# Second block of a two-block network: low parts of the weights and half of the position additions moved to GpSimd, and the stick-breaking mask moved from the weights to the scores

## The chip, the cores and the metric

The kernel runs on one core of a Trainium2 chip. The metric is the device time of one execution in microseconds (us), as the median of several runs. TensorE (PE, its weight loads PEld), VectorE (DVE), ScalarE (ACT), GpSimd (POOL) and SyncE (SP, which issues the DMAs) each run their own fixed list of instructions and wait for each other through semaphores.

## The reference, cut to what matters

One sequence of 512 rows and 1024 columns goes through two blocks. The first is a root-mean-square norm, sliding-window attention and a gated convolution, and a feed-forward layer. The second projects the normed rows to 33 groups of columns and runs three mixers on them, whose results are projected, added and normed once more. Of the second block, the parts that the change touches are these:

```
h = x @ w_in                                              # 33 weight tiles of 128 columns, the gates with 18
kc, vc: blocks = src[:, blk_idx] + cmp_pos                # 31 blocks of 32 rows, a step of 16
        gelu(blocks @ w1) @ w2                            # compressed keys, compressed values
...
mask = s_idx[None, :] < t[:, None]                        # stick-breaking: strictly earlier keys
log_rest = where(mask, log_sigmoid(-z), 0)
between = reverse cumulative sum of log_rest, moved by one
a = where(mask, exp(log_sigmoid(z) + between), 0)
o = a @ v
...
hgrn2: gated linear recurrence in chunks of 64, 6 heads in 3 pairs
```

## The kernel before, in words

Everything is held transposed, with columns on the 128 partitions and the 512 rows along the free dimension. Each product with a weight is made of three matmuls per 128 by 128 piece, since both sides are split into a high part and a low part of what the high part leaves: high by high, high by low, low by high. A weight tile is 128 partitions by 8 pieces of 128, fetched by SP as `raw`. `split_w` (L223) makes `wh` by a copy on ACT (L230) and `wl = raw - wh` by a subtraction on DVE (its helper `tt`, L138). `raw`, `wh` and `wl` have two buffers each. The class `Weights` (L237) loads four tiles and splits two tiles ahead of the product, `dense`, which takes one: 24 matmuls of 128x512 for a whole tile. `W2` (L704) is its instance for the second block's projection: 32 whole tiles and one of 128x8x18 for the gates.

The last norm of the first block is that of `norm3`, which stands ahead of the first product of `W2` that leaves its bank. Its squares are summed tile by tile on GpSimd by `Squares.add` (L328); then `rms_scale` multiplies the sum by a matrix of ones on PE into bank `gb` (`pgb<-nk,ones`) and DVE reads that (L315). At the same time `load_biasc` (L878) copies 24 small strided pieces of the bias on GpSimd. It stands in `compressed`, which then calls `blocks` (L880) for the compressed keys (`kc`) and for the compressed values (`vc`). `blocks` adds the position table to strided views of the projected tile: 8 additions of 64 partitions by 8 by 31 on DVE (L899) for each of the two. The products that read them are first-layer matmuls `pgb<-np,nk`.

Stick-breaking, `sticks` (L1071), handles two heads at a time in two calls (`bq`, `bk`, `bv` with c 0 and 1), each with two heads and three score tiles `zs` per head that hold the four column bands of the lower triangle (`ZP`). Per tile: scores on PE into bank `ga`, a copy on ACT, then `e = log(1+exp(z))` in three ACT steps and one DVE step; `strict` (L1069, GpSimd `affine_select`) sets `e` to 0 where the key is not strictly earlier than the query; ACT copies the high part (L1100), DVE the low part; PE sums it with the triangular matrix `trir`; DVE adds the sums to the scores; ACT takes the exponential (L1116); `strict` once more sets the same part of the result to 0; and `run(todo, ends)` issues the products with the values (`poa<-lv,gp`) behind the last of these (`ends`).

The recurrence (`recurrence`, pairs g0, g1, g2) is the part with the most DVE and ACT instructions; its products stand between those of the projection. The Tile framework's scheduler sets the order of all engines when the program is built, by its own estimate and by priorities: `split_w` asks for a priority ahead of its place (`offset=100`), `run` for a higher one (1000). So the order of every engine is fixed in the program, and a change in one place can move instructions in another.

Of the kernel before, what the change touches and what calls it, by code (L numbers as in the profile page):

```python
# [10 lines left out]
F32 = mybir.dt.float32  # L11
# [3 lines left out]
AF = mybir.ActivationFunctionType  # L15
ALU = mybir.AluOpType
AX = mybir.AxisListType

P = 128
# [3 lines left out]
NEG = -1e30  # L23
# [26 lines left out]
IN2 = {}  # L50
for _n, _c in (("nq", 3), ("kc", 0), ("vc", 0), ("ks", 0), ("vs", 0), ("kw", 0), ("vw", 0), ("bq", 2), ("bk", 2),
               ("bv", 2), ("gq", 3), ("gf", 3), ("gi", 3), ("z", 8)):
    for _i in range(max(_c, 1)):
# [4 lines left out]
ORDER = [("gf", 0), ("gq", 0), ("gi", 0), "ng", "kc", "vc", ("nq", 0), ("nq", 1), ("nq", 2), "ks", "vs", "kw", "vw",  # L58
         ("gf", 1), ("gq", 1), ("gi", 1), ("bq", 0), ("bk", 0), ("bv", 0), ("gf", 2), ("gq", 2), ("gi", 2),
         ("bq", 1), ("bk", 1), ("bv", 1)]  # L60
# [8 lines left out]
def tile_net(ctx, tc, a, out):  # L69
# [64 lines left out]
    def stt(o, i0, s, i1, op0, op1):  # L134
        V.scalar_tensor_tensor(o, i0, s, i1, op0, op1)  # L135

    def tt(o, i0, i1, op):
        V.tensor_tensor(o, i0, i1, op)  # L138
# [81 lines left out]
        nc.sync.dma_start(raw, src)  # L220
        return raw

    def split_w(raw, cuts=(0, 8)):  # L223
        nk, w = raw.shape[1], raw.shape[2]
        wh = wp.tile([P, 8, P], F32R, tag="wh", name=nm("wh"), bufs=2)[:, :nk, :w]
        wl = wp.tile([P, 8, P], F32R, tag="wl", name=nm("wl"), bufs=2)[:, :nk, :w]
        with tc.high_priority(offset=100):
            for c0, c1 in zip(cuts, cuts[1:]):
                c = slice(c0, min(c1, nk))
                A.copy(wh[:, c], raw[:, c])  # L230
                tt(wl[:, c], raw[:, c], wh[:, c].bitcast(F32), ALU.subtract)
        return wh, wl

    class Weights:


        def __init__(self, srcs):  # L237
            self.srcs, self.raw, self.w, self.n = srcs, [], [], 0

        def ahead(self, loads, splits):  # L240
            while len(self.raw) < min(loads, len(self.srcs)):
                self.raw.append(fetch(*self.srcs[len(self.raw)]))
            while len(self.w) < min(splits, len(self.raw)):
                self.w.append(split_w(self.raw[len(self.w)]))

        def take(self):
            n = self.n
# [89 lines left out]
    raw = raw_tile()  # L337
# [20 lines left out]
    def C(n):  # L358
        o, w = CM[n]
        return cst[:, o:o + w]  # L360
# [340 lines left out]
        lower_bounds()  # L701


    W2 = Weights([(a["w_gate"], 8, 18) if key == "ng" else (a["w_in_2"][IN2[key]], 8) for key in ORDER])  # L704
    cmi = cp.tile([P, 2, P], U8, tag="cmi", name="cmi")
    cmf = tl("nk")[:, 0:256]
    nc.sync.dma_start(cmf, a["cmask"])
# [169 lines left out]
                o = 31 + 128 * (3 - i)  # L877
                G.tensor_copy(v[:, h, 0:n], bias[h][:, o:o + 16 * (n - 1) + 1:16])  # L878

    def blocks(name, w1name, w2name):  # L880

        w1 = [np_().rearrange("p (k h) -> p k h", k=4) for _ in range(4)]
        for n in range(4):
            nc.sync.dma_start(w1[n], a[w1name][:, 4 * n:4 * n + 4])
        w2 = small(64)
        nc.sync.dma_start(w2, a[w2name])
        yield from need(name)
        src = pr[name]
        blks = [nk(), nk()]
        pos = S("pos").rearrange("p (r j) -> p r j", r=2)  # L890
        for n in range(2):
            G.memset(blks[n][:, 496:512], 0.0)
            blk = blks[n][:, 0:496].rearrange("p (j n) -> p j n", j=8)
            for g in range(2):
                s = src[64 * g:64 * g + 64]
                for par in range(2):
                    v = bass.AP(tensor=s.tensor, offset=s.offset + par + 16 * n,
                                ap=[list(s.ap[0]), [2, 8], [16, 31]])
                    last = V.tensor_tensor(  # L899
                        blk[64 * par:64 * par + 64, :, 31 * g:31 * g + 31], v,  # L900
                        pos[64 * g:64 * g + 64, par, 8 * n:8 * n + 8].unsqueeze(2).to_broadcast([64, 8, 31]), ALU.add,
                    )
        yield 0
        return w1, w2, blks, last
# [6 lines left out]
    def compressed():  # L911
        for h in range(3):
            G.memset(vcn[h].rearrange("p g d -> p (g d)"), 0.0)
        load_biasc()
        wk1, wk2, bk, e0 = yield from blocks("kc", "w_ck1", "w_ck2")
        wv1, wv2, bv, e1 = yield from blocks("vc", "w_cv1", "w_cv2")

        ps = bank("gb")
        todo = []
        for k in range(16):  # L920
            c = slice(62 * (k % 8), 62 * (k % 8) + 64)
            for r, w1, blks in ((0, wk1, bk), (64, wv1, bv)):
                todo.append(later(ps[r:r + 64, 0:P], blks[k // 8][:, c], w1[k // 4][:, k % 4], k == 0, k == 15))
        run(todo, [e0, e1])
        xy = nk()
        x, y, yT = (xy[:, P * n:P * n + P] for n in range(3))
        A.copy(x, ps[:, 0:P])
        tt(y, x, x, ALU.mult)
        V.tensor_scalar(y, y, 0.044715, 1.0, ALU.mult, ALU.add)
        tt(y, y, x, ALU.mult)  # L930
        V.tensor_scalar(y, y, -2.0 * math.sqrt(2.0 / math.pi), 80.0, ALU.mult, ALU.min)
        A.activation(y, y, AF.Exp)
        V.tensor_scalar(y, y, 1.0, None, ALU.add)
        V.reciprocal(y, y)
        tt(y, y, x, ALU.mult)
        yield 2.0
        ps = bank("gb")
        TE.transpose(ps[:, 0:P], y, ident)
        A.copy(yT, ps[:, 0:P])
        ps = bank("gb")  # L940
        for g in range(2):
            for r in (0, 64):
                mm(ps[r:r + 64, 32 * g:32 * g + 31], wk2, yT[:, 31 * g:31 * g + 31])
        kv = ps[:, 0:64].rearrange("p (g n) -> p g n", g=2)[:, :, 0:31]
        A.copy(kc2[:, :, 0:31], kv)
        tt(kc2[:, :, 31:62], kv, kc2[:, :, 0:31].bitcast(F32), ALU.subtract)
        yield 0.3
        ps = bank("gb")
        for g in range(2):
            for h in range(3):  # L950
                mm(ps[32 * h:32 * h + 31, 64 * g:64 * g + 64], yT[:, 64 + 31 * g:64 + 31 * g + 31], wv2)
        for h in range(3):
            A.copy(vcn[h][32 * h:32 * h + 31], ps[32 * h:32 * h + 31, 0:128])
        yield 0.5
        yield from need("ng", ("nq", 0), ("nq", 1), ("nq", 2))
        for i in range(4):
            pc = small(192)
            pv = pc.rearrange("p (h n) -> p h n", n=32)[:, :, 0:31]
            st = small(16)
            ps = bank("gb")  # L960
            for g in range(2):
                for h in range(3):
                    n = 64 * (3 * g + h)
                    mm(ps[:, n:n + 62], pr["nq", h][g][:, i * P:(i + 1) * P], kc2[:, g, 0:62])
            sv = ps[:, 0:384].rearrange("p (h n) -> p h n", h=6)
            tt(pv, sv[:, :, 0:31], biasc[i], ALU.add)
            tt(pv, pv, sv[:, :, 31:62], ALU.add)
            V.tensor_reduce(st[:, 0:6], pv, AX.X, ALU.max)
            tt(pv, pv, st[:, 0:6].unsqueeze(2).to_broadcast([P, 6, 31]), ALU.subtract)
            A.activation(pv, pv, AF.Exp)  # L970
            V.tensor_reduce(st[:, 6:12], pv, AX.X, ALU.add)
            V.reciprocal(st[:, 6:12], st[:, 6:12])
            tt(st[:, 6:12], st[:, 6:12], gate[:, i].rearrange("p (h b) -> p h b", b=3)[:, :, 0], ALU.mult)
            tt(pv, pv, st[:, 6:12].unsqueeze(2).to_broadcast([P, 6, 31]), ALU.mult)
            G.memset(pc.rearrange("p (h n) -> p h n", n=32)[:, :, 31:32], 0.0)
            yield 0.7
            ps = bank("gb")
            for g in range(2):
                TE.transpose(ps[0:96, g * P:(g + 1) * P], pc[:, 96 * g:96 * g + 96], ident)
            if i % 2 == 0:  # L980
                pch = tl("np")
            o = pch[:, 256 * (i % 2):256 * (i % 2) + 256]
            A.copy(o[0:96], ps[0:96, 0:256])
            pcT.append(o.rearrange("p (g t) -> p g t", g=2))
            yield 0.3
        done.add("cmp")
# [79 lines left out]
    ZW = [512, 512, 256]  # L1066

    def strict(t, o):
        return G.affine_select(t[:, o:o + P], t[:, o:o + P], [[1, P]], ALU.is_gt, 0.0, base=0, channel_multiplier=-1)  # L1069

    def sticks(cs):  # L1071
        for c in cs:
# [4 lines left out]
            for hh in range(2):  # L1077
# [5 lines left out]
                for b in range(3):  # L1083
# [12 lines left out]
                    stt(e, z, 0.0, e, ALU.max, ALU.add)  # L1096
                    for jb in range(4):
                        if ZP[jb][0] == b:
                            strict(e, ZP[jb][1])
                    A.copy(sh[b], e)  # L1100
                    tt(sl[b], e, sh[b].bitcast(F32), ALU.subtract)
                    yield 0.8
                for b in range(3):
# [9 lines left out]
                            mm(cb[:, o + n - n2:o + n], w, sh[b2][:, o2:o2 + n2], jj == jb, False)  # L1113
                            mm(cb[:, o + n - n2:o + n], w, sl[b2][:, o2:o2 + n2], False, jj == 3)
                    tt(zs[b], zs[b], cb[:, :ZW[b]], ALU.add)
                    A.activation(zs[b], zs[b], AF.Exp)  # L1116
                    for jb in range(4):
                        if ZP[jb][0] == b:
                            e = strict(zs[b], ZP[jb][1])
                            if hh == 1:  # L1120
                                ends.append(e)
                    yield 0.8
                both.append(zs)
            todo = []
# [366 lines left out]
```

## Time and profile before

| what | value |
|---|---|
| median of 3 runs | 1061.83 us (1061.65 to 1062.62) |
| the profiled execution | 1061.65 us |
| its span in the trace | 1059.8 us |
[...]
| PE busy | 97% |
| DVE busy | 66% |
| ACT busy | 46% |
| GpSimd busy | 4% |

The span is the time from the first to the last instruction in the trace; the execution's time holds 1.9 us more around it. Busy is the time in which an engine carries out an instruction. PE's busy share hides where it stands still: the view of waits sums up the idle time of an engine by what ended it.

### The profile page before, as it was taken

How to read it: one execution, taken by the hardware profiler on the slowest of the kernel's cores; microseconds unless marked ns; L12 is line 12 of the kernel's file. 1: busy time of each engine (PE TensorE's matmuls, PEld its weight loads, DVE VectorE, ACT ScalarE, POOL GpSimd, SP SyncE). 2: the span in 40 equal slices, each digit the busy share in tenths (PEclk: the TensorE clock that was granted, in tenths of full speed). 3: DMA queues.
4: the chain of work that ended last, by engine and by line, in shares of the span. 5: the costliest groups of instructions: out<-in, count | busy, mean ns of one | idle time of the engine just before them, and what ended most of it. 6: DMA issues, size and time to landing. Idle time of an engine off the chain costs nothing.

```text
span 1059.8 us, 14588 instructions
## 1 busy us (share of the span) xinstructions
PE 1028.5 (97%) x5689; PEld 835.7 (79%) x5689; DVE 704.3 (66%) x1307; ACT 485.6 (46%) x854; POOL 47.4 (4%) x93
## 2 busy tenths in 40 slices
PE   9999999999999999999999999998999999999997
PEld 7788888888888888888877888766777777777886
DVE  6886643356448767777763333497779788788847
ACT  5764443322345444444442223342455477478830
POOL 0000000000220000000000111200000011001100
PEclk9999999999999999999999999999999999999999
DMA  6212232233432333333336333610221111011232
GB/s 221 80 61 80 80 100 80 100 100 103 155 110 91 100 100 99 100 94 90 97 99 208 95 100 104 222 61 24 88 69 61 40 53 49 22 60 41 71 110 79
DMA packets 32800, 97.83 MB, mean 92 GB/s; under 512 B 4878, under 2 KB 5390, under 8 KB 32732
## 3 DMA queue, kind: packets, MB, share of 16 engines
q1 hardware_dynamic: 32732, 96.91, 28.9%
q8 instruction: 44, 0.72, 0.3%
q14 instruction: 24, 0.20, 0.1%
HBM read 94.77 MB, written 5.27 MB: 94 GB/s over the span
## 4 chain that ended last, share of the span: by engine, by line
PE 73%; DVE 14%; ACT 6%; DMA 2%; issue 2%; POOL 1%; SPq 1%; POOLq 0%; DVEq 0%; ACTq 0%
PE pm L141 44%; PE poa L141 12%; PE pob L141 11%; PE pgb L141 3%; PE pga L141 2%; DVE wl L138 2%; DVE lv L138 2%; DVE dk L138 2%; DVE hk L138 1%; ACT wh L230 1%; DMA raw<-in_w_down 1%; DVE r L138 1%; DVE nk L1010 1%; DVE nk L899 1%; DVE nk L997 1%
## 5 line engine op out<-in xcount | busy, mean ns | idle before, releaser
L141 PE MATMUL pm<-x,wh 128*128 128x512 f32 x1360 | 435.2, 397 | 1.9 <-ACT x L287 1.0
L141 PEld LDWEIGHTS pm<-x,wh 128*128 128x128 f32 x1360 | 252.0, 189 | 56.2 <-issue 4.9
L230 ACT CAST wh<-raw 128x1024 fp32r<-128x1024 f32 (+2 forms) x153 | 156.5, 1024 | 256.7 <-issue 102.5
L141 PE MATMUL pm<-x,wl 128*128 128x512 f32 x680 | 268.3, 395 | 0.0
L138 DVE TENSOR_TENSOR wl<-raw,wh 128x1024 fp32r<-128x1024 f32 (+2 forms) x153 | 182.0, 1190 | 88.0 <-ACT wh L230 85.0
L141 PEld LDWEIGHTS pm<-x,wl 128*128 128x128 f32 x680 | 128.2, 188 | 27.5 <-issue 1.9
L141 PE MATMUL pob<-x,wh 128*128 128x512 f32 (+1 forms) x208 | 64.9, 392 | 0.0
L141 PE MATMUL poa<-x,wh 128*128 128x512 f32 x208 | 64.9, 393 | 0.0
L141 PE MATMUL pm<-np,wh 128*128 128x512 f32 x152 | 46.8, 389 | 0.0
L138 DVE TENSOR_TENSOR dk<-pm,rs 128x512 f32<-128x512 f32 x43 | 29.5, 685 | 25.9 <-PE pm L141 25.8
L141 PEld LDWEIGHTS poa<-x,wh 128*128 128x128 f32 x208 | 39.1, 188 | 9.0 <-issue 1.0
L138 DVE TENSOR_TENSOR nk<-pm,rs 128x512 f32<-128x512 f32 x35 | 24.0, 686 | 32.1 <-PE pm L141 31.9
L141 PEld LDWEIGHTS pob<-x,wh 128*128 128x128 f32 (+1 forms) x208 | 37.6, 181 | 9.6 <-issue 0.2
L141 PE MATMUL poa<-x,wl 128*128 128x512 f32 x104 | 40.6, 390 | 0.1
L141 PE MATMUL pob<-x,wl 128*128 128x512 f32 (+1 forms) x104 | 40.5, 389 | 0.0
L141 PEld LDWEIGHTS pm<-np,wh 128*128 128x128 f32 x152 | 28.5, 188 | 5.9
L1003 ACT ACTIVATE nk<-nk,q 128x128 f32<-128x128 f32 (+3 forms) x48 | 26.5, 554 | 11.3 <-DVE q L1001 11.2
L141 PE MATMUL pm<-np,wl 128*128 128x512 f32 x76 | 29.6, 389 | 0.0
L997 DVE CUSTOM_DVE_ANT_0 nk<-pgb,bi 128x128 f32<-128x128 f32 (+3 forms) x48 | 22.6, 485 | 6.8 <-PE pgb L141 6.6
L135 DVE SCALAR_TENSOR_TENSOR nk<-nk,smt,nk 128x511 f32<-128x511 f32 (+2 forms) x33 | 24.7, 748 | 1.3 <-ACT nk L469 0.8
L135 DVE SCALAR_TENSOR_TENSOR nk<-dk,smt,nk 128x511 f32<-128x511 f32 (+2 forms) x33 | 24.7, 747 | 0.8 <-ACT nk L469 0.3
L135 DVE SCALAR_TENSOR_TENSOR dk<-nk,smt,dk 128x511 f32<-128x511 f32 (+1 forms) x32 | 23.9, 748 | 1.6 <-ACT dk L469 0.8
(508 smaller groups left out, 1664.1 us busy)
## 6 DMA issues: line engine op xcount, KB each, us to landing
raw<-in_w_in SPq DMA_DIRECT2D x65, 512.0 KB, 3.4
raw<-in_w_up SPq DMA_DIRECT2D x44, 512.0 KB, 3.5
raw<-in_w_down SPq DMA_DIRECT2D x16, 512.0 KB, 3.5
raw<-in_w_br SPq DMA_DIRECT2D x8, 512.0 KB, 3.5
raw<-in_w_out SPq DMA_DIRECT2D x8, 512.0 KB, 3.5
raw<-in_w_out SPq DMA_DIRECT2D x16, 256.0 KB, 2.6
raw<-in_w_down SPq DMA_DIRECT2D x8, 384.0 KB, 3.2
d<-d SPq DMA_DIRECT2D x6, 512.0 KB, 6.7
```

Of the source, the lines that this page charges most:

```text
L135: V.scalar_tensor_tensor(o, i0, s, i1, op0, op1)
L138: V.tensor_tensor(o, i0, i1, op)
L141: return TE.matmul(o, l, r, start=start, stop=stop)
L230: A.copy(wh[:, c], raw[:, c])
L899: last = V.tensor_tensor(blk[64 * par:64 * par + 64, :, 31 * g:31 * g + 31], v, pos[64 * g:64 * g + 64, par, 8 * n:8 * n + 8].unsqueeze(2) ...
L997: V.tensor_tensor_reduce(pb[:, 0:Wd_], s[:, 0:Wd_], bias[h][:, T - Wd_:T], 1.0, -3e38, ALU.add, ALU.max, st[:, g:g + 1])
L1003: A.activation(pbs[g][:, 0:Wd_], pbs[g][:, 0:Wd_], AF.Exp, bias=st[:, 2 + g:3 + g], accum_out=st[:, 4 + g:5 + g])
L1010: V.tensor_scalar(pbs[g][:, 0:Wd_], pbs[g][:, 0:Wd_], st[:, 8 + g:9 + g], None, ALU.mult)
```

## The change

Three edits, all in the second block:

- `split_w` has a flag `aside`, which `W2` sets: the low part of a weight tile is then subtracted on GpSimd in two halves of four pieces (128x512 elements each) in place of one subtraction of 128x1024 on DVE. That is 33 DVE instructions gone and 66 on GpSimd added (64 of 128x512 and 2 for the gate tile). The weights of the first block and of the last projection stay as they were.
- `blocks` is given the engine of its additions: GpSimd for `kc`, DVE for `vc` as before.
- `sticks`: the diagonal band of `e` is masked on DVE, by multiplying with `ntri + 1` (ntri holds -1 on and below the diagonal and 0 elsewhere); GpSimd sets the scores themselves to -1e30 in the same place, behind the step that reads them for `e` and ahead of the step that adds the sums; the second selection, behind the exponential, is gone, and `ends` are the exponentials on ACT. That is 16 selections fewer on GpSimd (32 before), and 16 DVE instructions of 128x128 more.

```diff
-    def split_w(raw, cuts=(0, 8)):
+    def split_w(raw, cuts=(0, 8), aside=False):
...
                 A.copy(wh[:, c], raw[:, c])
-                tt(wl[:, c], raw[:, c], wh[:, c].bitcast(F32), ALU.subtract)
+                if not aside:
+                    tt(wl[:, c], raw[:, c], wh[:, c].bitcast(F32), ALU.subtract)
+            if aside:
+                for c in (slice(0, nk // 2), slice(nk // 2, nk)):
+                    G.tensor_tensor(wl[:, c], raw[:, c], wh[:, c].bitcast(F32), ALU.subtract)
...
-    W2 = Weights([(a["w_gate"], 8, 18) if key == "ng" else (a["w_in_2"][IN2[key]], 8) for key in ORDER])
+    W2 = Weights([(a["w_gate"], 8, 18) if key == "ng" else (a["w_in_2"][IN2[key]], 8) for key in ORDER], aside=True)
...
-    def blocks(name, w1name, w2name):
+    def blocks(name, w1name, w2name, eng):
...
-                    last = V.tensor_tensor(
+                    last = eng.tensor_tensor(
...
-        wk1, wk2, bk, e0 = yield from blocks("kc", "w_ck1", "w_ck2")
-        wv1, wv2, bv, e1 = yield from blocks("vc", "w_cv1", "w_cv2")
+        wk1, wk2, bk, e0 = yield from blocks("kc", "w_ck1", "w_ck2", G)
+        wv1, wv2, bv, e1 = yield from blocks("vc", "w_cv1", "w_cv2", V)
...
     def strict(t, o):
-        return G.affine_select(t[:, o:o + P], t[:, o:o + P], [[1, P]], ALU.is_gt, 0.0, base=0, channel_multiplier=-1)
+        G.affine_select(t[:, o:o + P], t[:, o:o + P], [[1, P]], ALU.is_gt, NEG, base=0, channel_multiplier=-1)
...
                     stt(e, z, 0.0, e, ALU.max, ALU.add)
                     for jb in range(4):
                         if ZP[jb][0] == b:
-                            strict(e, ZP[jb][1])
+                            d = e[:, ZP[jb][1]:ZP[jb][1] + P]
+                            stt(d, C("ntri"), 1.0, d, ALU.add, ALU.mult)
+                            strict(z, ZP[jb][1])
...
                     tt(zs[b], zs[b], cb[:, :ZW[b]], ALU.add)
-                    A.activation(zs[b], zs[b], AF.Exp)
-                    for jb in range(4):
-                        if ZP[jb][0] == b:
-                            e = strict(zs[b], ZP[jb][1])
-                            if hh == 1:
-                                ends.append(e)
+                    e = A.activation(zs[b], zs[b], AF.Exp)
+                    if hh == 1:
+                        ends.append(e)
```

The edits also move instructions that they do not name. In all, DVE's list goes from 1309 to 1284 instructions and GpSimd's from 98 to 156; those of PE (5033), ACT (776) and SP (227) keep their length, and SP's keeps its order. Lines behind `split_w` have numbers that are 5 higher in the changed kernel, and those behind `sticks` 4.

**GpSimd around the third norm.** `bi` are the bias tiles and `np` the two tiles that the pieces are copied into; `nk<-nk,dk` is the last addition of the squares. Before, the list has behind the cast of a mask 20 copies (the first four and the last four are shown), then the addition:

```order
L708 CAST cmi<-nk_5070 128x256
L878 COPY np_5549<-bi_5085 128x7
L878 COPY np_5549<-bi_5085 128x15
...
L878 COPY np_5563<-bi_5093 128x23
L878 COPY np_5563<-bi_5093 128x31
L328 TENSOR_TENSOR nk_4423<-nk_4423,dk_5063 128x512
```

In the changed kernel:

```order
L713 CAST cmi<-nk_5070 128x256
L235 TENSOR_TENSOR wl_5107<-raw_5098,wh_5106 128x512 x2
L883 COPY np_5556<-bi_5085 128x7
...
L883 COPY np_5570<-bi_5087 128x31
L235 TENSOR_TENSOR wl_5112<-raw_5100,wh_5111 128x512 x2
L883 COPY np_5556<-bi_5089 128x7
...
L883 COPY np_5570<-bi_5093 128x31
L333 TENSOR_TENSOR nk_4423<-nk_4423,dk_5063 128x512
```

Two weight tiles have come in ahead of the addition: both halves of the first one ahead of all copies, and both halves of the second one between the 8th and the 9th of the 20 copies.

**PE in the middle of the second recurrence pair.** `pm<-x,wh` and `pm<-x,wl` are a projection tile's products, `pga<-lv` products of the pair g1. Before:

```order
L141 MATMUL pm_6759<-x_4790,wl_6653 128x512
L141 MATMUL pm_6759<-x_4883,wh_6652 128x512
L141 MATMUL pm_6759<-x_4884,wh_6652 128x512
L141 MATMUL pm_6759<-x_4883,wl_6653 128x512
L141 MATMUL pga_6809<-lv_6619 128x128
L141 MATMUL pga_6810<-lv_6619 128x128
```

In the changed kernel:

```order
L141 MATMUL pm_6667<-x_4976,wh_6558 128x512
L141 MATMUL pm_6667<-x_4977,wh_6558 128x512
L141 MATMUL pm_6667<-x_4976,wl_6559 128x512
L141 MATMUL pm_6667<-x_5059,wh_6558 128x512
L141 MATMUL pga_6829<-lv_6637 128x128
L141 MATMUL pga_6830<-lv_6637 128x128
```

The same products of g1 stand behind 22 matmuls of one weight tile now (`wh_6558`), and behind 18 of the tile after it before (`wh_6652`), so 24 + 18 - 22 = 20 matmuls of 128x512 come later in PE's list than they did. In the same way the products of g2 stand 16 matmuls earlier, and the first-layer products of the compressed keys and values 12.

**DVE ahead of the compressed products.** `nk982` is the projected `kc`, `nk1006` the projected `vc`; `hk` copies belong to the local attention. Before:

```order
L899 TENSOR_TENSOR nk999_5587<-nk982_5488,smt_75 64x8x31
L138 TENSOR_TENSOR wl1014_5670<-raw970_5416,wh1013_5669 128x1024
L899 TENSOR_TENSOR nk999_5587<-nk982_5488,smt_75 64x8x31
L899 TENSOR_TENSOR nk1000_5588<-nk982_5488,smt_75 64x8x31
L1235 COPY_PREDICATED hk973_5434<-cmi_5069,pga990_5516 128x512
L1235 COPY_PREDICATED hk974_5436<-cmi_5069,pga991_5517 128x512
L899 TENSOR_TENSOR nk1000_5588<-nk982_5488,smt_75 64x8x31 x3
L138 TENSOR_TENSOR nk1006_5609<-pm984_5496,rs3_5066 128x512
L899 TENSOR_TENSOR nk1007_5611<-nk1006_5609,smt_75 64x8x31 x4
L899 TENSOR_TENSOR nk1008_5612<-nk1006_5609,smt_75 64x8x31 x4
```

In the changed kernel:

```order
L1239 COPY_PREDICATED hk973_5440<-cmi_5069,pga980_5470 128x512
L1239 COPY_PREDICATED hk974_5442<-cmi_5069,pga981_5471 128x512
L1239 COPY_PREDICATED hk973_5440<-cmi_5069,pga990_5523 128x512
L1239 COPY_PREDICATED hk974_5442<-cmi_5069,pga991_5524 128x512
L138 TENSOR_TENSOR nk1006_5616<-pm984_5502,rs3_5066 128x512
L904 TENSOR_TENSOR nk1007_5618<-nk1006_5616,smt_75 64x8x31 x4
L904 TENSOR_TENSOR nk1008_5619<-nk1006_5616,smt_75 64x8x31 x4
```

The additions for `kc` and the weight tile have left DVE's list here; the 8 for `vc` stand at its end as before.

## Rows read from the trace of the kernel before

**Rows 1.** The page: span, busy time of each engine, chain that ended last.

```profile
span 1059.8 us, 14588 instructions
...
PE 1028.5 (97%) x5689; PEld 835.7 (79%) x5689; DVE 704.3 (66%) x1307; ACT 485.6 (46%) x854; POOL 47.4 (4%) x93
...
PE 73%; DVE 14%; ACT 6%; DMA 2%; issue 2%; POOL 1%; SPq 1%; POOLq 0%; DVEq 0%; ACTq 0%
```

**Rows 2.** Waits of PE: tile waited for <- releaser: us, times, longest.

```profile
PE pgb L141 <- DVE nk L899: 3.2, 1, 3.2
...
PE pga L141 <- ACT hk L1100: 2.5, 3, 1.0
...
PE poa L141 <- POOL hk L1069: 2.3, 2, 1.2
...
PE pga L141 <- DVE hk L1235: 1.5, 2, 1.3
...
PE pgb L141 <- POOL nk L328: 1.4, 1, 1.4
...
PE poa L141 <- DVE wl L138: 0.5, 1, 0.5
```

**Rows 3.** Stretches: length, then PE, PEld, DVE, ACT, POOL, PEclk, DMA, GB/s.

```profile
620.00:640.00 20.00, 20.00 (x90) 16.55 (x89) 5.99 (x6) 5.15 (x6) 1.78 (x1) 1.00 0.31 97
...
678.20:682.00 3.80, 3.78 (x15) 2.79 (x16) 2.39 (x3) 2.23 (x4) 0.86 (x9) 1.00 0.07 26
...
700.00:720.00 20.00, 19.26 (x241) 14.66 (x239) 19.85 (x51) 5.17 (x11) 0.00 (x0) 1.00 0.20 58
...
728.60:731.90 3.30, 3.30 (x36) 3.30 (x34) 0.00 (x0) 0.00 (x0) 0.00 (x0) 0.50 0.00 0
...
800.00:820.00 20.00, 19.32 (x237) 14.73 (x235) 19.89 (x61) 11.70 (x29) 0.00 (x0) 1.00 0.17 54
820.00:840.00 20.00, 18.77 (x178) 14.83 (x180) 16.64 (x35) 9.57 (x21) 0.00 (x0) 1.00 0.08 27
```

**Rows 4.** Timeline at the third norm: start us, us, instruction [idle before <-releaser].

```profile
672.30 1.23 DVE L138 TENSOR_TENSOR wl<-raw,wh 128x1024 fp32r<-128x1024 f32 x1 [0.17 <-ACT wh L230]
...
672.73 4.21 POOL L878 COPY np<-bi 128x7 f32<-128x7 f32 x20 [12.01 <-DMA bi<-d]
...
672.73 0.85 POOL L878 COPY np<-bi 128x7 f32<-128x7 f32 x1 [12.01 <-DMA bi<-d]
...
676.90 1.26 POOL L328 TENSOR_TENSOR nk<-nk,dk 128x512 f32<-128x512 f32 x1
...
678.22 1.12 PE L141 MATMUL pgb<-nk,ones 128*128 128x512 f32 x2 [1.37 <-POOL nk L328]
```

**Rows 5.** DVE from 668 to 1000 us, groups by shape: busy us, mean ns.

```profile
L138 DVE TENSOR_TENSOR wl<-raw,wh 128x1024 fp32r<-128x1024 f32 x32 | 39.2, 1224 | 8.9 <-ACT wh L230 8.8
...
L899 DVE TENSOR_TENSOR nk<-nk,smt 64x248 f32<-64x248 f32 x16 | 9.1, 571 | 0.3
```

**Rows 6.** Timeline, an earlier addition of the squares beside DVE.

```profile
658.48 0.75 DVE L135 SCALAR_TENSOR_TENSOR x<-r,smt,x 128x512 fp32r<-128x512 f32 x1
...
658.60 1.78 POOL L328 TENSOR_TENSOR nk<-nk,nk 128x512 f32<-128x512 f32 x1 [13.18 <-ACT nk L324]
```

**Rows 7.** Timeline ahead of the compressed products.

```profile
723.41 4.64 DVE L899 TENSOR_TENSOR nk<-nk,smt 64x248 f32<-64x248 f32 x8
...
728.10 1.15 PE L141 MATMUL pgb<-np,nk 128*64 128x128 f32 x12 [3.21 <-DVE nk L899]
```

**Rows 8.** Timeline of stick-breaking: two selections of e, and the last selection.

```profile
866.21 1.89 POOL L1069 TENSOR_SCALAR_AFFINE_SELECT dk<-dk 128x128 f32<-128x128 f32 x2 [7.90 <-DVE dk L135]
...
896.08 0.47 POOL L1069 TENSOR_SCALAR_AFFINE_SELECT hk<-hk 128x128 f32<-128x128 f32 x1
...
896.33 1.30 DVE L138 TENSOR_TENSOR wl<-raw,wh 128x1024 fp32r<-128x1024 f32 x1
...
896.61 1.31 PE L141 MATMUL poa<-lv,gp 128*64 128x128 f32 x20 [1.14 <-POOL hk L1069]
```

More of the change, by code (lines that the diff above doesn't have):

```diff
@@ L230, in split_w, with __init__ @@
                 A.copy(wh[:, c], raw[:, c])
-                tt(wl[:, c], raw[:, c], wh[:, c].bitcast(F32), ALU.subtract)
+                if not aside:
[3 more added lines that the diff above has]
+                    G.tensor_tensor(wl[:, c], raw[:, c], wh[:, c].bitcast(F32), ALU.subtract)
         return wh, wl
     class Weights:
-        def __init__(self, srcs):
+        def __init__(self, srcs, aside=False):
             self.srcs, self.raw, self.w, self.n = srcs, [], [], 0
+            self.aside = aside
         def ahead(self, loads, splits):
@@ L243, in ahead @@
             while len(self.w) < min(splits, len(self.raw)):
-                self.w.append(split_w(self.raw[len(self.w)]))
+                self.w.append(split_w(self.raw[len(self.w)], aside=self.aside))
         def take(self):
```

## Prediction

> **What bounds the kernel now.** I read the page first. PE is busy for 97% of the span and holds 73% of the chain that ended last; DVE, the next, holds 14%, GpSimd 1% [rows 1]. None of the edits takes a matmul away. So they can gain only what PE idles in the second block, plus what a low clock costs there; and they can lose whatever new idle time they make. Next I read PE's waits. Five entries touch the edited parts: 3.2 us for the position additions, 2.5 us for ACT's copy of `e`, 2.3 us for the last selections, 1.5 us for DVE in the local attention, and 1.4 us for the last addition of the squares [rows 2]. The reader should see that they sum to 10.9 us, about 1% of the span, and that PE waited for a low part of the weights once only, for 0.5 us. The third view is that of stretches: DVE, 66% busy over all, is busy for 19.85 of 20 us from 700 to 720 and for 36.5 of 40 us from 800 to 840 [rows 3]. There DVE is the engine that sets the pace, and there it matters what GpSimd does beside it. The timelines come last, for what an instruction costs alone and beside another engine.
>
> **GpSimd and DVE together.** The addition of two 128x512 tiles on GpSimd took 1.26 us [rows 4]. The same addition took 1.78 us when a DVE instruction with two inputs had started 0.12 us ahead of it and ran 0.75 us [rows 6]: 0.52 us longer, close to the 0.63 us for which that instruction still ran. The first small copy on GpSimd took 0.85 us beside DVE's subtraction of a weight tile, the other 19 took (4.21 - 0.85) / 19 = 0.18 us each [rows 4]. A last selection that stretched to 0.47 us was followed by a DVE subtraction of 1.30 us where its like take 1.22 [rows 5, 8]. So the two take turns, and DVE was held too, if only by 0.08 us here, behind a selection on a quarter of the columns.
>
> [...]
>
> What a half of a weight tile on GpSimd (128x512, two inputs) costs DVE is the unknown. Nothing in the trace has it; its ends are 8 x 0.08 = 0.64 us, if what DVE lost behind a selection grows with the two-input columns read, and 1.26 us, if DVE stands for the whole of it. In a stretch in which DVE has pauses, it may also cost nothing. I take 0.8 us, nearer to the row in which DVE itself was seen held: 1.6 us per tile, where 1.22 us is removed. Where DVE is dense, the move is then worth -0.4 us per tile to DVE, not +1.2.
>
> **The third norm.** The 20 copies and the addition stand in one queue, and PE waits 1.37 us for the addition [rows 4]. In the changed order two halves stand between the copies: + 2 x 1.26 us, - 0.67 us which the first copy no longer loses to DVE's subtraction, so the addition ends 1.9 us later and PE idles 3.2 us. I take nothing for the first tile's halves, since GpSimd sat idle for 12.01 us ahead of the copies. [...] Term: **+3.5** (bounds +1.9 without a fall, +4.8 if the addition meets a two-input DVE instruction too).
>
> **The compressed products.** PE's longest wait ends with the 8 additions for `vc`, 4.64 us on DVE [rows 7], which stay. What comes off DVE ahead of them is 8 additions for `kc`, 8 x 0.57 = 4.6 us, and four weight tiles, 4.9 us [rows 5]. What comes in is DVE held: four times 1.6 us, and 8 additions on half the partitions with 248 elements, which I put at half of a tile's half each, 0.4 us: 3.2. That is 9.5 off and 9.6 on, so **0**. The end at which DVE is not held takes off the wait of 3.2 us, the slow clock behind it, 1.6 us, and DVE's wait in the local attention, 1.3 of its 1.5: -6.1. The other end is the new order: the products stand 12 matmuls earlier, 12 x 20/90 = 2.7 us [rows 3], and would wait that much longer.
>
> **The recurrence.** The order puts g1's products 20 matmuls earlier, 20 x 20/90 = 4.4 us, as if DVE had become faster. From 800 to 840 us three weight tiles lie on DVE: 36.5 - 3 x 1.22 + 3 x 1.6 = 37.7 us of 40. DVE has no room to deliver earlier, so PE would wait for the 4.4 us; but other products stand around it which fill part of it, and I take half: +2.2. For g2, 16 matmuls or 3.6 us earlier, where stretches are less dense, I take a smaller share, +1.0. Term: **+3.2** (bounds 0 if DVE keeps up, 8.0 if neither does).
>
> **Stick-breaking.** The last selections ended two waits of PE, 2.3 us in all [rows 2]; 1.14 us of them is the one at 896.61, behind a select that itself took 0.47 us [rows 8]. With `ends` on ACT both waits go: -2.3. The selection of `e`, 1.89 us for two beside DVE [rows 8], leaves the path to ACT's copy, for which PE waited 2.5 us; in its place come two DVE instructions on 128 columns each, by a quarter of the 0.75 us of a 512-column one [rows 6] 0.2 us apiece. DVE has other work queued there, so I take half of the wait: -1.2. The selections of the scores now stand between two steps of ACT and PE that take longer, and I cost them at nothing; without that cover each is 0.3 to 1.2 us. Term: **-3.5** (bounds -5.0 and -1.0).
>
> **Late weights.** GpSimd needs 2.5 us and more for what DVE did in 1.22, behind up to 4 us of copies. Splits run two tiles ahead, some 10 us of PE, and only once did PE wait for one [rows 2]. That cover hides it: 0. If it is gone, a tile costs 1.3 us and more.
>
> **Sum.** 3.5 + 0 + 3.2 - 3.5 = +3.2 us against the profiled execution's 1061.65, which is 0.2 us below the median of the runs: **1064.9 us**, with a range of its own of 1062 to 1068.
>
> **Rivals.** (1) *DVE is hardly held*, under some 0.6 us per half: then each tile gives DVE time back and the dense stretches run as the order wants. 1061.65 + 1.9 - 6.1 - 3.5 = 1054.0. For it: DVE lost only 0.08 us in rows 8, and a pause of DVE takes up what is held for nothing. Against it: GpSimd visibly waits for DVE, so something is shared. (2) *Balance*: no fall of the clock at the norm and no wait from the order: 1061.65 + 1.9 - 3.5 = 1060.0. (3) *DVE held for the whole GpSimd instruction*: by rows 6, turned round, 2.5 us per tile against 1.22 removed. The new order is then waited for in full: 3.5 - 3.5 + 4.4 + 3.6 + 2.7 = +10.7, 1072.3. [...] (4) That the scheduler leaves the work where it was is excluded: the order rows show it moved.
>
> **Chances.** Forecast 0.33, (1) 0.29, (2) 0.25, (3) 0.13. About 0.2%, 2.1 us, is what a measurement can tell from no change, so "same" is 1059.7 to 1064.0. Faster: (1) and a fifth of (2), whose centre lies just inside that band: 0.29 + 0.05 = 0.34. Slower: (3), and seven tenths of the forecast's case, whose centre lies above 1064.0: 0.13 + 0.23 = 0.36. Same: the rest, 0.30. The range takes in (1) with a margin of one and (3) likewise: 1053 to 1073; cases of both signs hold most of it, and the forecast's own range stands above.
>
> **What would show it.** In the profile after: PE's idle time ahead of the ones product near 3.2 us with a stretch at clock 0.5 behind it (right) or under 2 us (wrong). Halves of `wl` on GpSimd at 1.3 to 2 us, and DVE instructions with two SBUF inputs longer than before by up to that; if their means are as before, rival (1) holds. A wait of PE for the position additions still near 3 us, waits in the recurrence grown by 2 to 4 us; no wait of PE for a selection. What would make it wrong above all: that DVE's time per instruction does not grow where GpSimd works, or that PE waits for `wl`.

## The result, and the profile after

The changed kernel takes 1091.2 us (median of 5 runs, 1090.35 to 1094.85), the kernel before 1061.74: a ratio of 1.0283, interval 1.0270 to 1.0295, or 29.5 us more. The forecast was 1064.9 with a range of 1053 to 1073, so it had the sign and missed the size by far.

The page of the changed kernel: span and busy time of each engine.

```profile
span 1090.5 us, 14666 instructions
...
PE 1040.7 (95%) x5689; PEld 839.2 (77%) x5689; DVE 702.9 (64%) x1282; ACT 485.8 (45%) x854; POOL 133.8 (12%) x151
```

Against [rows 1], DVE's busy time has fallen by 1.4 us only, from 704.3, though the 33 subtractions have left it. On a page of averages that looks like balance; PE's waits tell more. Waits of PE in the changed kernel:

```profile
PE pgb L984 <- DVE q L138: 4.1, 3, 1.6
PE pga L141 <- DVE lv L138: 4.1, 6, 1.7
PE pga L141 <- DVE dk L138: 3.6, 4, 2.0
PE pgb L141 <- POOL nk L333: 3.1, 1, 3.1
PE pgb L141 <- issue: 3.1, 1, 3.1
PE pgb L1025 <- DVE nk L1015: 2.2, 4, 0.7
```

No wait for a selection is left, and none for a low part on GpSimd. The new and grown ones are for DVE, spread over attention, the recurrence and stick-breaking. The gaps between PE's matmuls from 655 us on, counted from 0.03 us, sum to 36.4 us against 18.6 before. That is 17.8 of the 30.7 us by which the span grew. A part of the rest is the granted clock, in the mean 0.991 of full speed over the span against 0.995 before, which a stretch by stretch view shows:

```profile
680.00:700.00 20.00, 18.82 (x74) 12.67 (x74) 10.74 (x20) 8.07 (x16) 7.23 (x11) 0.91 0.26 80
700.00:720.00 20.00, 16.67 (x198) 11.18 (x198) 18.97 (x46) 6.70 (x14) 6.01 (x7) 0.91 0.14 50
...
880.00:900.00 20.00, 17.47 (x102) 13.52 (x101) 16.42 (x49) 12.50 (x28) 6.57 (x7) 0.91 0.17 54
```

The kernel before had one such stretch of 20 us between its norm and its last stretch, at 720 to 740; the changed one has these three and that one. In each of them the clock stood at 0.50 for some 3.3 us; the traces of the two kernels show no other levels than 0.50 and 1.00. Half of such a stretch is lost: where the third one held 32 products of 128x128, the 1.6 us behind it held 33, at a mean clock of 0.97. The four stretches:

```profile
681.10:684.40 3.30, 3.30 (x8) 2.25 (x7) 0.78 (x2) 1.35 (x3) 2.49 (x3) 0.50 0.11 40
701.60:704.90 3.30, 3.30 (x6) 1.20 (x7) 2.55 (x7) 0.53 (x2) 0.00 (x0) 0.50 0.00 0
735.70:739.00 3.30, 3.30 (x32) 3.30 (x34) 0.00 (x0) 0.00 (x0) 0.00 (x0) 0.50 0.00 0
892.70:896.00 3.30, 3.10 (x8) 2.46 (x8) 2.81 (x20) 1.95 (x7) 0.42 (x1) 0.50 0.49 161
```

Three more of them cost some 5 us. The other 8 us or so were not followed.

Next the instructions themselves. DVE from 668 us on by shape, busy us and mean ns, in the kernel before:

```profile
L138 DVE TENSOR_TENSOR dk<-pm,rs 128x512 f32<-128x512 f32 x22 | 15.0, 682 | 4.4 <-PE pm L141 4.4
...
L138 DVE TENSOR_TENSOR lv<-hk,gp 128x256 f32<-128x256 f32 x30 | 11.5, 417 | 0.7 <-ACT hk L1154 0.6
L138 DVE TENSOR_TENSOR np<-dk,np 64x512 fp32r<-64x512 f32 x14 | 9.6, 685 | 0.4
...
L1001 DVE TENSOR_SCALAR q<-q 128x2 f32<-128x2 f32 x24 | 4.0, 167 | 0.3
```

The same in the changed kernel:

```profile
L138 DVE TENSOR_TENSOR lv<-hk,gp 128x256 f32<-128x256 f32 x30 | 15.1, 544 | 0.6 <-ACT hk L1158 0.6
L138 DVE TENSOR_TENSOR dk<-pm,rs 128x512 f32<-128x512 f32 x22 | 15.1, 685 | 12.0 <-PE pm L141 11.9
L138 DVE TENSOR_TENSOR np<-dk,np 64x512 fp32r<-64x512 f32 x14 | 14.6, 1043 | 2.1 <-ACT np L424 1.8
...
L1006 DVE TENSOR_SCALAR q<-q 128x2 f32<-128x2 f32 x24 | 9.3, 387 | 0.3
```

The one among these that reads a PSUM bank (`dk<-pm,rs`) takes what it took, 685 ns in the mean after 682. Many of those that read SBUF alone take longer in the mean, `lv<-hk,gp` by a third and `np<-dk,np` by a half, and the one on two columns takes 387 ns in place of 167. Over all groups that have as many instructions before as after, DVE lengthened by 33 us. One place shows how. The changed kernel near 891 us, GpSimd, DVE, ACT and PE:

```profile
889.61 2.62 POOL L235 TENSOR_TENSOR wl<-raw,wh 128x512 fp32r<-128x512 f32 x2 [3.00 <-ACT wh L230]
...
891.03 1.22 DVE L1006 TENSOR_SCALAR q<-q 128x2 f32<-128x2 f32 x1
892.16 0.68 DVE L138 TENSOR_TENSOR gp<-pm,rs 128x512 f32<-128x512 f32 x1
...
892.28 0.61 ACT L1008 ACTIVATE nk<-nk,q 128x384 f32<-128x384 f32 x1 [1.59 <-DVE q L1006]
...
892.89 1.22 PE L141 MATMUL pm<-x,wh 128*128 128x512 f32 x2 [1.30 <-DVE gp L138]
```

GpSimd's second half runs from 890.92 to 892.22. DVE's instruction on two columns starts 0.11 us behind it and ends 0.03 us behind its end: 1.22 us for what takes 0.17. ACT's exponential waits for it for 1.59 us, the next DVE instruction stands behind it, and PE waits for that one for 1.30 us. So this DVE instruction is held until the GpSimd one has ended, as no row of before had shown. Of the 24 of its kind, seven began while a half ran, and each of the seven ended 0.02 to 0.03 us behind the end of that half.

### The profile page after: what moved, and what is told of

Its sections match the earlier page's. It is cut to its first block, busy times and chain, and to the rows that moved or that the text cites. A ratio compares the mean times of both kernels' runs of the same rounds, so it can differ in the third digit from the quotient of the medians.

```text
span 1090.5 us, 14666 instructions
## 1 busy us (share of the span) xinstructions
PE 1040.7 (95%) x5689; PEld 839.2 (77%) x5689; DVE 702.9 (64%) x1282; ACT 485.8 (45%) x854; POOL 133.8 (12%) x151
## 5 line engine op out<-in xcount | busy, mean ns | idle before, releaser
L138 DVE TENSOR_TENSOR wl<-raw,wh 128x1024 fp32r<-128x1024 f32 (+3 forms) x120 | 142.5, 1188 | 79.5 <-ACT wh L230 76.6
L235 POOL TENSOR_TENSOR wl<-raw,wh 128x512 fp32r<-128x512 f32 (+1 forms) x66 | 88.8, 1366 | 204.4 <-ACT wh L230 169.1
L138 DVE TENSOR_TENSOR dk<-pm,rs 128x512 f32<-128x512 f32 x43 | 29.5, 687 | 33.4 <-PE pm L141 33.2
L333 POOL TENSOR_TENSOR dk<-dk,nk 128x512 f32<-128x512 f32 x5 | 8.5, 1696 | 292.0 <-ACT nk L329 292.0
L333 POOL TENSOR_TENSOR nk<-nk,dk 128x512 f32<-128x512 f32 x3 | 4.8, 1607 | 283.3 <-DVE wl L138 270.1
```

Of the source, the lines that this page charges most:

```text
L235: G.tensor_tensor(wl[:, c], raw[:, c], wh[:, c].bitcast(F32), ALU.subtract)
L333: G.tensor_tensor(self.acc, self.acc, s, ALU.add)
```

## Experiments

Three theories. (1) DVE held by what GpSimd reads. (2) The new order: the scheduler takes DVE to be lighter and puts products earlier than they can be ready. (3) The 16 masks on DVE.

**The parts alone.** First the mask on the scores, with `aside=True` and `G` taken back:

```
-    W2 = Weights([...], aside=True)
+    W2 = Weights([...])
-        ... blocks("kc", "w_ck1", "w_ck2", G)
+        ... blocks("kc", "w_ck1", "w_ck2", V)
```

> The mask on the scores alone; low parts of the weights and all position additions on DVE. If what costs 29 us is DVE held by GpSimd's halves of weight tiles (theory 1), nothing of it is here: 1058 to 1061 us, the -3.5 of the prediction or a part of it. If it is the new order of the products (theory 2): within 3 us of before, since only 211 of PE's 5033 instructions stand elsewhere. If it is the 16 masks on DVE (theory 3): 1070 or more.

Measured: 1059.84 us, 0.9975 of before (0.9965 to 0.9985). A gain of 2.7 us; theory 3 falls. PE's wait for selections is gone, ACT's one wait for a mask on DVE is 1.7 us long.

Then the keys' additions alone (`G` kept, the other two parts as before):

> Only the 8 additions of the compressed keys moved to GpSimd. Theory 1: the additions leave DVE (-4.6 us) and hold it for some 4 us: 1060 to 1064. Theory 2: 18 of PE's instructions stand elsewhere, so no change. Theory 3: no change. A rise of over 4 us would say that small strided additions hold DVE far more than a weight half.

Measured: 1061.62 us, 0.9992 (0.9983 to 1.0000). No difference.

Then the low parts alone (`aside=True` kept, the other two as before):

> Only the low parts of the second block's weights moved to GpSimd. Theories 1 and 2: nearly all of the 29 us, 1088 to 1095. Theory 3: 1075 or less.

Measured: 1102.28 us, 1.0376 (1.0363 to 1.0389), above the range expected. All of the loss is here, and 11 us more than the changed kernel has. So beside the weight halves the other two parts are worth more than alone. The selections explain little of that: ACT waits for them no longer than in the kernel before, and PE 2.8 us against 2.3 [rows 2]. ACT's waits for selections before:

```profile
ACT hk L1100 <- POOL dk L1069: 4.1, 5, 2.0
...
ACT hk L1100 <- POOL hk L1069: 2.6, 4, 1.2
```

Waits for selections in this kernel, the first of ACT, the second of PE:

```profile
ACT hk L1105 <- POOL dk L1074: 4.7, 6, 1.8
...
PE poa L141 <- POOL hk L1074: 2.8, 2, 1.5
```

In sum the 11 us are PE's gaps, 42.5 us against 36.4 in the changed kernel, and the clock, at 0.50 for 23.9 us against 13.7 between 655 and 1040 us, half of it lost. Why they grow by so much is open.

**Order or hold, with the order kept.** The changed kernel, writing only:

```
-                    G.tensor_tensor(wl[:, c], raw[:, c], wh[:, c].bitcast(F32), ALU.subtract)
+                    G.memset(wl[:, c].bitcast(F32), 0.0)
```

> The changed kernel with each subtraction on GpSimd replaced by a write of zeros into the same half (the low parts of the second block's weights are left out). GpSimd then only writes; the order of PE, DVE and ACT is that of the changed kernel but for 20, 25 and 35 instructions. Theory 1: DVE is free of 40 us and not held: 1050 to 1062. Theory 2: PE waits for products that stand too early: 1080 or more.

Measured: 1057.88 us, 0.9967 (0.9955 to 0.9979). With the changed kernel's order and DVE not held there is no loss, but a gain of 3.5 us, hardly more than the mask alone. Theory 2 falls. DVE is at 668.5 us of busy time, the two-column instruction back at 169 ns, and no stretch of 20 us from 640 to 1040 has a clock below 1.00:

```profile
PE 1031.2 (98%) x5689; PEld 835.1 (79%) x5689; DVE 668.5 (63%) x1282; ACT 485.9 (46%) x854; POOL 77.6 (7%) x151
...
L1006 DVE TENSOR_SCALAR q<-q 128x2 f32<-128x2 f32 x24 | 4.1, 169 | 0.3
```

**The other way round: the order of before, with the hold.** DVE keeps its subtractions, and GpSimd does them again:

```
                 tt(wl[:, c], raw[:, c], wh[:, c].bitcast(F32), ALU.subtract)
+            if ghost:
+                for c in (slice(0, nk // 2), slice(nk // 2, nk)):
+                    G.tensor_tensor(raw[:, c], raw[:, c], wh[:, c].bitcast(F32), ALU.subtract)
```

> The kernel before, with the subtractions of the weights left on DVE, and done a second time on GpSimd in halves over the raw tile, where nobody reads them. DVE's own work and the order are those of before (34 of PE's 5033 instructions and 28 of DVE's 1309 stand elsewhere). Theory 1 (DVE held by GpSimd's reads): DVE's instructions with two inputs in SBUF lengthen by some 30 us in all, with no relief: 1085 to 1110. Theory 2 (order): 1060 to 1066.

Measured: 1107.69 us, 1.0427 (1.0409 to 1.0445).

The same with `G.memset(raw[:, c], 0.0)` in the last line:

> The same list as the run before on every engine, word for word, but GpSimd writes zeros over the half in place of reading two tiles. Theory 1 with the hold on reads: 1060 to 1064. If any GpSimd instruction that writes holds DVE, or if the later release of the raw tile is what costs: above 1070.

Measured: 1066.50 us, 1.0039 (1.0025 to 1.0054). Between the two lies only GpSimd's instruction: one reads two tiles and takes 1.50 us in the mean, the other writes zeros in 0.53. PE multiplies the same numbers in both. They are 41.2 us apart. DVE's busy times on their pages, first of the run that reads, then of the one that writes:

```profile
PE 1042.1 (94%) x5689; PEld 840.3 (76%) x5689; DVE 746.3 (67%) x1307; ACT 486.3 (44%) x854; POOL 143.7 (13%) x159
```

```profile
PE 1030.8 (97%) x5689; PEld 835.2 (78%) x5689; DVE 705.9 (66%) x1307; ACT 486.0 (46%) x854; POOL 79.2 (7%) x159
```

That is 40.4 us of DVE's time, so theory 1 holds with the order of before as well. The second run also stands 4.8 us above before, a little more than expected. Its trace shows about half of that at the third norm, where PE's wait for the addition of the squares is 2.3 us (1.4 before) and the clock behind it falls, as it had not before:

```profile
PE pgb L141 <- POOL nk L332: 2.3, 1, 2.3
```

```profile
681.00:684.20 3.20, 3.20 (x9) 2.42 (x9) 2.96 (x5) 1.35 (x3) 0.98 (x2) 0.50 0.09 35
```

For the rest, candidates are the raw tiles' later release and the 34 moved instructions; they were not told apart.

**The size of the hold.** One GpSimd instruction per tile, then eight:

```
-                for c in (slice(0, nk // 2), slice(nk // 2, nk)):
+                for c in (slice(0, nk),):
...
+                for c in [slice(i, i + 1) for i in range(nk)]:
```

> The changed kernel with one GpSimd instruction of 128x1024 per weight tile in place of two halves; the order of PE, DVE and ACT is the same. If DVE is held for a whole GpSimd instruction, single DVE instructions wait up to 2.5 us, half as many of them: 1088 to 1100, with a maximum of some 2.7 us for an instruction on 128x2. If the two share in proportion to the data, nothing changes: 1089 to 1093, and no single wait is longer.

Measured: 1102.03 us, 1.0376 (1.0358 to 1.0394), 2 us above the range expected of a hold.

> The same with eight GpSimd instructions of 128x128 per weight tile. If DVE is held for a whole GpSimd instruction, a wait is at most some 0.35 us, GpSimd waits between its pieces in turn, and DVE lengthens by less: 1065 to 1080. If they share in proportion to the data: 1089 to 1093, or more for the fixed cost of eight instructions.

Measured: 1080.75 us, 1.0176 (1.0158 to 1.0193), just above what was expected of a hold. The two-column instruction with its shortest, median and longest time, in the changed kernel, with one instruction per tile, and with eight:

```profile
L1006 DVE TENSOR_SCALAR q<-q x24: 147/169/1246, 795.4 to 1008.4; 128x2 f32<-128x2 f32 x24
```

```profile
L1006 DVE TENSOR_SCALAR q<-q x24: 150/167/2220, 798.4 to 1015.7; 128x2 f32<-128x2 f32 x24
```

```profile
L1006 DVE TENSOR_SCALAR q<-q x24: 154/169/422, 787.8 to 996.6; 128x2 f32<-128x2 f32 x24
```

The median does not move; the longest, 1.25, 2.22 and 0.42 us, follows the length of GpSimd's instruction, 1.40, 2.42 and 0.59 us in the mean. That is a hold, not a share. In eight pieces GpSimd pays: a piece of 128x128 took 586 ns in the mean, so 4.7 us per tile where one of 128x1024 took 2.4.

```profile
L235 POOL TENSOR_TENSOR wl<-raw,wh 128x1024 fp32r<-128x1024 f32 x32 | 77.3, 2415 | 213.1 <-ACT wh L230 176.3 <-PE pgb L141 15.3 <-PE pm L141 14.2
```

```profile
L235 POOL TENSOR_TENSOR wl<-raw,wh 128x128 fp32r<-128x128 f32 x256 | 141.1, 586 | 152.8 <-ACT wh L230 122.2 <-PE pgb L141 14.8 <-issue 11.0
```

**One input.** `G.tensor_copy(wl[:, c], raw[:, c])` in place of the subtraction:

> The changed kernel with each half's subtraction replaced by a copy of the raw half on GpSimd (the low parts are wrong by that: the high part is left in). GpSimd reads one tile instead of two; the lists are those of the run with zeros written. If any read of GpSimd holds DVE for the length of its instruction, then in proportion to that length: a copy of some 0.6 us instead of 1.26, about half of the 33 us of lengthening, 1068 to 1078. If only a second input of GpSimd meets DVE: 1056 to 1062.

Measured: 1063.09 us, 1.0017 (1.0007 to 1.0028), between the two expectations. A copy took 677 ns in the mean on GpSimd, half of the subtraction, but DVE's busy time rose by a sixth of what it does there: 673.8 us against 668.5 with zeros and 702.9 with subtractions. So here a GpSimd instruction that reads one input holds DVE too, by much less than in proportion to its length. Its trace shows that fewer DVE instructions meet one, and each for less: 19 beside a copy are over 0.06 us longer than the median of their like in the run with zeros, by 0.34 us in the mean, where beside the subtractions 48 are, by 0.74. Whether the second input adds anything beyond the length was not tried apart.

These five kernels have the same list of instructions on DVE but for 25 places, so they can be set side by side (a held instruction counts as busy):

| GpSimd per weight tile | DVE busy, us | time, us |
|---|---|---|
| writes zeros, two halves | 668.5 | 1057.88 |
| copies, two halves | 673.8 | 1063.09 |
| subtracts, eight pieces | 688.7 | 1080.75 |
| subtracts, two halves (the change) | 702.9 | 1091.2 |
| subtracts, one piece | 711.9 | 1102.03 |

From the first row to the last: 44.2 us of time for 43.4 us by which DVE is held. In these kernels a microsecond of hold goes with one of the kernel's. That is a sum, and not each hold passed on: from the first row to the change, PE's gaps from 655 us on grow from 12.5 us to 36.4, which is 23.9 of the 34.4 us of hold, and the four stretches at clock 0.50 shown above, which the first row does not have, cost some 7 us more.

**The third norm.** The first two weight tiles back on DVE:

```
-                self.w.append(split_w(self.raw[len(self.w)], aside=self.aside))
+                self.w.append(split_w(self.raw[len(self.w)], aside=self.aside and len(self.w) >= 2))
```

> The changed kernel with the low parts of the first two weight tiles back on DVE; nothing else in any engine's list moves. By the term for the third norm, the wait ahead of the ones product falls from 3.1 to 1.4 us and the stretch at half clock behind it goes: 3.3 to 3.5 us faster than the changed kernel, 1087 to 1089. If the lost time there is hidden anyway: 1090 to 1092.

Measured: 1088.95 us, 1.0258 (1.0243 to 1.0274), 2.3 us less than the changed kernel by the medians, with intervals that just touch. The wait is back to 1.4 us from 3.1, and the clock behind it stays at 1.00, where half of 3.3 us had been lost: by these rows the term was there as priced, 3.4 us. The whole kernel does not show it so cleanly. The clock falls elsewhere too: behind a wait of 1.62 us in the attention here and not in the changed kernel, and not at 892.7 us here as it did there. That the two profiled spans are 3.4 us apart is therefore in part chance. The clock at the norm and at that place in the attention in this run:

```profile
680.60:684.40 3.80, 3.80 (x19) 3.11 (x17) 2.55 (x7) 1.27 (x3) 1.60 (x2) 1.00 0.21 80
...
776.90:780.30 3.40, 3.40 (x13) 2.92 (x13) 2.25 (x8) 1.05 (x3) 0.00 (x0) 0.50 0.40 146
```

In the changed kernel, GpSimd and PE at the norm (the clock behind it is the first of the four stretches above):

```profile
673.26 1.31 POOL L883 COPY np<-bi 128x7 f32<-128x7 f32 x8 [1.85 <-DMA bi<-d]
674.53 2.99 POOL L235 TENSOR_TENSOR wl<-raw,wh 128x512 fp32r<-128x512 f32 x2
677.47 1.84 POOL L883 COPY np<-bi 128x7 f32<-128x7 f32 x12
679.28 1.25 POOL L333 TENSOR_TENSOR nk<-nk,dk 128x512 f32<-128x512 f32 x1
...
680.59 1.64 PE L141 MATMUL pgb<-nk,ones 128*128 128x512 f32 x2 [3.13 <-POOL nk L333]
```

**A version that beats both.** The change without its weight halves (`aside=True` taken back):

> The changed kernel without its largest part: the mask on the scores and the keys' additions on GpSimd, all low parts on DVE. If the two parts add up, 0.9975 and 0.9992 give 0.9967 of before: 1058 to 1060. If the additions on GpSimd meet the scheduler's order in another way: up to 1064.

Measured: 1058.71 us, 0.9975 (0.9964 to 0.9985), the same as the mask alone. And with the last addition of the norm's squares moved from GpSimd's queue to DVE:

```
-        def add(self, src):
+        def add(self, src, eng=None):
...
-                G.tensor_tensor(self.acc, self.acc, s, ALU.add)
+                (eng or G).tensor_tensor(self.acc, self.acc, s, ALU.add)
...
-            sqs.add(hs[e])
+            sqs.add(hs[e], V if e == 7 else None)
```

> The run before with the last addition of the third norm's squares on DVE instead of GpSimd, ahead of which 20 copies stand. DVE was idle for 4.2 us there, so the addition starts as soon as the last square is there: the wait of 1.4 us goes, 1 to 1.4 us faster than that run, 1057 to 1059. If the square itself is as late as the copies are: no difference.

Measured: 1056.76 us, 0.9961 (0.9949 to 0.9974): 4.1 us faster than before. In its trace DVE does the addition and PE no longer waits ahead of the ones product:

```profile
675.28 0.68 DVE L333 TENSOR_TENSOR nk<-nk,dk 128x512 f32<-128x512 f32 x1
...
676.84 1.02 PE L141 MATMUL pgb<-nk,ones 128*128 128x512 f32 x2
```

The intervals of the last two runs overlap, so the last step's 1.4 us, the wait that is gone, is read from the trace, not from the times.

## Why the prediction was wrong

- **The step that failed** is the unit price of a tile set against the subtraction it removes, "-0.4 us per tile to DVE", and its use in two dense stretches alone, with the words that in a stretch with pauses "it may also cost nothing". Seven tiles were counted, and net. The hold per half was even less than taken: (702.9 - 668.5) / 64 = 0.54 us in the place of 0.8, below the 0.6 us at which rival (1) was to decide, and still the time did not go rival (1)'s way. But it counted wherever a half met a DVE instruction, dense stretch or not, with nothing set against it: 34.4 us of hold in the place of a net -0.4 us for each of seven tiles, and 33.3 us of time (1091.2 - 1057.88).
- **What was removed was worth next to nothing.** The run that writes zeros has both DVE's subtractions and the hold gone, 35.8 us less DVE than before, and gains 3.5 us, of which the mask alone gives 2.7. The rows of before said so: PE had waited for a low part once, for 0.5 us [rows 2], and that was at 572 us, in the first block, where it stands in the changed kernel too. I had read those rows as cover for a later subtraction, and not as the price of the one that was taken off. A subtraction of a weight is done ahead and can wait; a hold meets whichever DVE instruction comes, those of a chain too, as at 891 us. That this difference makes the two prices is argued from that place and from the runs' sums; not every hold was followed.
- **The norm** came as worked out in the rows: idle 3.13 us (3.2 forecast), 0.50 granted for 3.3 us behind it. The clock's part of the term, 1.6 us, is half of the 3.30 us at 0.50 that the kernel before had behind its wait of 3.21 us [rows 3, 7]. The run that takes it back gained 2.3 us by the medians, with a clock fall elsewhere that the forecast (3.5) did not have. Falls of the clock behind new waits elsewhere were in no term, and there were two, at 701.6 and 892.7 us.
- **The compressed products**: the wait stayed, as forecast; 3.07 us. But the 8 additions for `vc`, which I had left at 4.64 us, took 6.05 beside a weight tile:

```profile
728.96 2.75 POOL L235 TENSOR_TENSOR wl<-raw,wh 128x512 fp32r<-128x512 f32 x2 [2.05 <-ACT hk L1250]
...
729.49 6.05 DVE L904 TENSOR_TENSOR nk<-nk,smt 64x248 f32<-64x248 f32 x8
...
735.64 2.76 PE L141 MATMUL pgb<-np,nk 128*64 128x128 f32 x23 [3.07 <-issue]
```

- **The order** (+3.2) was the wrong cause. The same order costs nothing where DVE is not held.
- **Stick-breaking** had sign and about the size: -2.7 by itself, -3.5 forecast, and the waits for selections went. The masks on DVE, put at 0.2 us each, took 0.44 in the mean for 12 of the 16 in the changed kernel:

```profile
L135 DVE SCALAR_TENSOR_TENSOR dk<-cst,dk 128x128 f32<-128x128 f32 x12 | 4.9, 435 | 0.0
```

- **Late weights** at 0 was right for the change: no row of PE's waits names a low part from GpSimd.
- **Rival (3)** named the mechanism, the hold for a whole instruction, with a chance of 0.13; but its price went through the order (10.7 us), and not through the sum of the holds.

## What to carry to other kernels

Ask of work that is moved off an engine whether anybody waited for it; where nobody did, its time is no credit. Where the engine that it moves to holds the first one, count the hold over all its instructions, not only over those in the dense stretches. Here the whole of it came back as time, through PE's waits and the clock behind them; elsewhere that has to be measured. What cost least here beside a busy DVE was a GpSimd instruction that only writes (DVE busy for 668.5 us), then one with a single input (673.8); two inputs cost most (688.7 to 711.9), and cutting them into pieces shortened the longest hold of the instruction on 128x2 (2.22 us to 0.42) but lengthened GpSimd's own time (2.4 us per tile to 4.7).

## What the runs showed of the hardware that was not expected

The hold is not for large instructions alone: one on 128x2 took up to 1.25 us beside a half, 2.22 beside a whole tile and 0.42 beside an eighth, with a median of 0.17 in all three. It has one input tile (`q<-q`), so two inputs on DVE's side are not needed for it; those of L1015, with one tile and a column of factors, were held too: four that began beside a running half took 1.33 to 1.46 us, where the longest before took 0.51. But one input in SBUF is not enough either: 7 of the 24 reciprocals on 128x2 began while a half was running, with up to 1.2 us of it left, and none took over 0.17 us.

```profile
L1011 DVE RECIPROCAL q<-q x24: 148/160/167, 797.0 to 1015.6; 128x2 f32<-128x2 f32 x24
```

The instruction with a PSUM input, `dk<-pm,rs`, was not lengthened (682 ns before, 685 in the changed kernel). Zeros written by GpSimd at 536 ns each left DVE's instructions nearly as they were: 169 ns for the one on 128x2 after 167, and 0.69 us for the longest of L1015 after 0.51.
